# A segment mean over sorted ids: probes and gathers ordered later in the queues, id sums fewer rows ahead

## The chip, the core and the metric

The kernel runs on one core of a Trainium2 chip. The metric is the device time of one execution in microseconds (us). A core has five engines with a queue each: TensorE (PE), VectorE (DVE), ScalarE (ACT), GpSimd (POOL) and SyncE (SP), which here only issues transfers. The transfers of all queues run on the core's 16 DMA engines.

## The reference

```python
n, num_segments = 10_000_000, 10000
data = randn(n).astype(float32)
segment_ids = sort(randint(0, num_segments, n))          # int64

sums = zeros(num_segments); counts = zeros(num_segments)
np.add.at(sums, segment_ids, data)
np.add.at(counts, segment_ids, 1)
return sums / maximum(counts, 1)
```

The ids are sorted, so each segment is one contiguous run of about 1,000 elements. Data is 40 MB; the ids would be 80 MB, and the kernel does not read them all.

## The kernel before

**Tiling.** Each of the 128 partitions holds 78,125 consecutive elements, worked on as 90 rows of 875 (the last has 250). A row holds at most one place where the id changes, or a general path is taken at the end (it is not, with this data). For each row the kernel needs the sum of all its elements (T), the place of the change (KK), and the sum of the elements before that place (A). The segment sums then come from scans over these per-row numbers.

**The steps of a row, and where they run.**
- *Probes* (load_probes, L156, on SP): every 175th id, 8 bytes each, loaded for a group of six rows at once; 15 groups, 128 x 30 ids each.
- *Data* (load_data, L163, on SP): tiles of two rows, 875 KB; 18 buffers. Before a buffer is loaded anew SP waits for its readers.
- *First look* (L253, DVE): once a group; five or six small steps find from the probes which window of 175 ids of each row holds the change, and write its index (IDX). It ends with the six gathers of the group.
- *Gather* (L299, POOL): an indirect load of the window's ids, 128 x 175, one for each row, into GT, a ring of 18.
- *Id sum* (add_ids, L310, ACT): adds the ids of one window. Rows 87 to 89 are summed together on DVE (add_ids_late, L316).
- *Second look* (L322, DVE): turns a group's id sums into KK.
- *Total* (L333, ACT): adds up a row's data. *Split* (L339, DVE): adds up the data before KK.

**The order** is written out by hand. A loop over r from -40 to 89 (L846) emits the work, and each queue runs its part in this order. At each r come: the probe loads that are X_PROBE + X_DATA rows ahead, the data loads that are X_DATA rows ahead, id sums up to X_SUM rows ahead of the total, the total and split of row r, and then all steps that `put(r, steps, every)` has listed under `after[r]`, `every` of them a row from r on. So on SP only the order of probe and data loads counts: the probes of group g stand just before the tile of rows 6g-14 and 6g-13. A first look stands after row 6g-12, its second look after row 6g-1. SP's loads each wait also for the one eight loads before, since eight completion semaphores are used in turn.

**The late work** also hangs on `put`. Counts, sums, select and table (L556, L586, L651, L660) turn rows of T, A and KK into segment means for parts of the rows; keys (L454) and edges_of (L440) prepare ids; check, single and verdict (L485, L538, L546) test that the fast path holds; pick (L688) makes masks, on DVE for rows 62 to 77 and on POOL for the rest; spread (L739) multiplies by these masks, total_of (L751) adds them up, weights (L713) and finish (L757) close. The sums and spread of rows 62 to 77 stand after row RM = 78, those of rows 78 to 83 after row RE = 84 and the one after it, the rest after row 88. The last first look (rows 84 to 89) stands after row 72, together with counts of rows 62 to 77.

The lines that place the looks and the id sums:

```python
put(a - 1, second_look(a, b))                                   # L792
put(max(bounds[g] - X_LOOK, 0), first_look(g), 5)               # L795
while r >= -1 and gs < min(r + 1 + X_SUM, IDS):                 # L864
    add_ids(gs)
```

Of the kernel before, what the change touches and what calls it, by code (L numbers as in the profile page):

```python
# [22 lines left out]
NR = 90  # L23
# [4 lines left out]
NX = NR + E  # L28
FAR = float(1 << 18)
GROUPS = [6] * 15  # L30
X_PROBE = 14
X_DATA = 26
X_LOOK = 12
X_SUM = 7
RING = 18
IDS = 87
NO = 79
SHIFT = 6
ND = 2 * SHIFT + 1
# [2 lines left out]
R1 = 8 * M1 - 2  # L42
R2 = NR + 4
RM = 78
RE = 84
C1, CA, C2 = 37, 70, 51


# [69 lines left out]
def kernel(  # L118
# [6 lines left out]
    nc = tc.nc  # L125
# [13 lines left out]
    ppool = ctx.enter_context(tc.tile_pool(name="ppool", bufs=1, space=bass.MemoryType.PSUM))  # L139

    ctx.enter_context(tc.manual_schedule())


    pr = cpool.tile([P, NR + 1, K], I64, name="pr")
# [171 lines left out]
    def add_ids_late(r):  # L316
        n, q = NR - r, r % RING
        nc.vector.tensor_reduce(  # L318
            out=GS[:, r:NR], in_=gt32[:, q : q + n, 0 : 2 * W : 2], axis=AX.X, op=ALU.add
        )  # L320

    def second_look(a, b):  # L322
        def s1():
            nc.vector.scalar_tensor_tensor(  # L324
                out=KK[:, a:b], in0=YY[:, a:b], scalar=float(S // K), in1=GS[:, a:b],
                op0=ALU.mult, op1=ALU.subtract,
            )
            if b == NR:
                nc.vector.tensor_add(out=KK[:, NR - 1 : NR], in0=KK[:, NR - 1 : NR], in1=tl)

        return [s1]
# [35 lines left out]
    pb = cpool.tile([P, NO - C2, R2 - RM], FP32, name="pb")  # L367
# [86 lines left out]
    def keys(a, b):  # L454
        def s1():
            if a == 0:
                nc.vector.tensor_add(out=base1, in0=VI[:, 0:1], in1=pin)

        def s2():
            v = VI[:, a:b] if b <= NR else V[:, a:b]  # L460
            nc.vector.tensor_scalar(
                out=KEY[:, PAD + a : PAD + b], in0=v, scalar1=base1[:, 0:1], scalar2=None, op0=ALU.subtract
            )
            if b <= NR:
                edges(a, b)
            if a == 0:
                nc.vector.tensor_sub(out=delta, in0=sp, in1=base1)

        def s3():
            if b <= NR:  # L470
                nc.vector.tensor_scalar(
                    out=NB[:, a:b], in0=BT[:, a:b], scalar1=1.0, scalar2=None, op0=ALU.not_equal
                )
            if a == 0:
                nc.vector.tensor_scalar(
                    out=dm, in0=jj[:, 0:ND], scalar1=delta[:, 0:1], scalar2=None, op0=ALU.is_equal
                )

        def s4():
            if b <= NR:  # L480
                positions(a, b)

        return [s1, s2, s3, s4]
# [204 lines left out]
    def pick(e, o, c0, n, a, b):  # L688

        w = b - a  # L690

        def s1():
            c = min(b, NR)
            e.tensor_scalar(
                out=KL[:, a - R1 : c - R1], in0=VI[:, a:c], scalar1=sp[:, 0:1], scalar2=None, op0=ALU.subtract
            )
            if c < b:
                e.tensor_scalar(
                    out=KL[:, c - R1 : b - R1], in0=V[:, c:b], scalar1=sp[:, 0:1], scalar2=None,
                    op0=ALU.subtract,  # L700
                )

        def s2():
            k, j = view(KL[:, a - R1 : a - R1 + 1], [[0, n], [1, w]]), view(jj[:, c0 : c0 + 1], [[1, n], [0, w]])
            if e is nc.vector:
                e.tensor_tensor(out=o, in0=k, in1=j, op=ALU.is_equal)  # L706
            else:
                e.tensor_tensor(out=o, in0=k, in1=j, op=ALU.subtract)
                e.tensor_scalar(out=o, in0=o, scalar1=0.0, scalar2=None, op0=ALU.is_equal)  # L709

        return [s1, s2]
# [68 lines left out]
    def put(r, steps, every=1):  # L780
        for i, f in enumerate(steps):
            after[r + i // every].append(f)
# [3 lines left out]
    after[-1] += second_look(0, GROUPS[0])  # L786
    for a, b in zip(bounds[1:], bounds[2:]):
        if b == NR:
            put(a - 2, second_look(a, IDS))
            put(a - 1, [lambda: add_ids_late(IDS)] + second_look(IDS, b), 2)  # L790
        else:
            put(a - 1, second_look(a, b))  # L792
    for g in range(HEAD, NG):
        if g < NG - 1:
            put(max(bounds[g] - X_LOOK, 0), first_look(g), 5)  # L795
# [1 line left out]
    def mixed(p, q):  # L797
        out = []
        for i in range(max(len(p), len(q))):
            out += p[i : i + 1] + q[i : i + 1]  # L800
        return out
# [15 lines left out]
    put(41, counts(0, Q1), 2)  # L817
    put(45, sums(0, Q1) + select(0, H1) + table(0, H1, tab), 2)
    put(52, [lambda: nc.sync.dma_start(out=out2d[0:SHIFT, :].rearrange("n u -> u n"), in_=tab[0:1, 0:SHIFT])])
    put(56, keys(48, 72)[1:], 2)  # L820
    put(59, counts(Q1, R1), 2)
    put(R1 - 1, mixed(sums(Q1, R1), select(H1, M1)) + table(H1, M1, tab), 2)
    put(64, place(0, T1, tab, [(0, C1, ND + 1, OUT[:, 0:C1]), (C1, T1, ND + 1, xa[:, 0 : T1 - C1, RM - R1])]))
    put(67, mixed(keys(72, RE)[1:], pick(nc.vector, pa[:, :, 0 : RM - R1], C1, CA - C1, R1, RM)), 2)
    put(69, check())
    look = bounds[NG - 1] - X_LOOK
    put(RM - 11, pick(nc.gpsimd, pb[:, :, 0 : RE - RM], C2, NO - C2, RM, RE), 2)
    put(look, mixed(first_look(NG - 1), counts(R1, RM)), 99)
    put(look, pick(nc.gpsimd, pb[:, :, RE - RM :], C2, NO - C2, RE, R2), 99)
    put(look + 1, mixed(edges_of(RE, NR), []), 99)  # L830
    put(look + 2, single(RE, NR, bad[:, 2 * NX + 8 :]) + verdict()[:1], 99)
    put(look + 3, verdict()[1:])
    after[look + 4].append(lambda: verdict_reg.append(nc.values_load(badi[0:1, 0:1], min_val=0, max_val=1)))
    put(RM, sums(R1, RM, False) + spread(R1, RM, pa[:, :, 0 : RM - R1], xa[:, :, 0 : RM - R1], CA - C1, nc.gpsimd), 4)
    put(RM + 4, total_of(xa[:, 0 : C2 - C1, :], OUT[:, C1:C2])
        + total_of(xa[:, C2 - C1 :, :], add[:, 0 : CA - C2, nb]), 2)
    put(RE, mixed(counts(RM, R2), sums(RM, RE, False)), 99)
    put(RE + 1, mixed(spread(RM, RE, pb[:, :, 0 : RE - RM], add[:, :, 0 : RE - RM], NO - C2), weights()), 99)
    put(NR - 2, sums(RE, R2, False, NR - 1)
        + spread(RE, R2, pb[:, :, RE - RM :], add[:, :, RE - RM : nb], NO - C2) + total_of(add, most), 99)  # L840
    assert max(after) <= NR - 1

    pnext = 0
# [2 lines left out]
    for r in range(-X_PROBE - X_DATA, NR):  # L846
        while pnext < NG and bounds[pnext] <= r + X_PROBE + X_DATA:
            load_probes(pnext)
            pnext += 1
            if pnext == 1:  # L850
                load_data(0)
                nt = 1
        while nt < NT and 2 * nt <= r + X_DATA:
            load_data(nt)
            nt += 1
        if r == -X_DATA:
            nc.scalar.dma_start(
                out=snt[0 : P - 1, :],
                in_=segment_ids[D : N].rearrange("(p d) -> p d", d=D)[:, 0:1],
            )  # L860
        if r == -1:
            for f in after[r][: 5 * HEAD]:
                f()
        while r >= -1 and gs < min(r + 1 + X_SUM, IDS):  # L864
            add_ids(gs)
            gs += 1
        if r == -1:
            for f in after[r][5 * HEAD :]:
                f()
        if r >= 0:  # L870
            total(r)
            split(r)
            for f in after[r]:
                f()
# [31 lines left out]
```

## Time and profile before

| what | us |
|---|---|
| median of 4 runs (lowest, highest) | 192.76 (192.18, 193.32) |
| the profiled execution | 191.72 |
| its span, first to last instruction | 189.9 |
| DVE busy | 141.6 (75%) |
| ACT busy | 135.2 (71%) |
| POOL busy | 99.0 (52%) |
| PE busy | 1.6 (1%) |
| one split of 875 elements, DVE | 1.12 |
| one total, ACT (with the read of its sum) | 0.93 + 0.19 |
| one id sum, ACT (with the read of its sum) | 0.36 + 0.19 |
| one gather's issue, POOL | 1.00 |

The page divides the span into 40 slices of 4.75 us; a digit is the busy share of a slice in tenths, 9 being 90% or more. The DMA row is the mean over 16 engines. In the list of waits a line reads: who waited, for whom, total us, times, longest. In the timeline a line reads: start, us, engine, line, operation, output and inputs with their shapes, and in brackets the idle time before it and what ended it. A DMA issued by POOL stands in the timeline with the time POOL needs to issue it; the landing comes later.

### The profile page before, as it was taken

The numbers are of one execution on the slowest core, as the hardware profiler recorded it, in microseconds if no ns is written. First come the engines' busy times: TensorE is split into PE (matmuls) and PEld (weight loads), VectorE is DVE, ScalarE is ACT, GpSimd is POOL, SyncE is SP. The second block draws the span as 40 slices with busy tenths as digits, with TensorE's granted clock in tenths as the row PEclk, the third lists the DMA queues.
The fourth block names the chain that finished last, engine by engine and source line by source line (L and its number), as shares of the span: only waits on it lengthen the run. The fifth ranks groups of instructions, "written<-read, shape, count | busy, mean of one in ns | idle before, by whom it ended". The sixth has DMA issues, their size and how long they took to land.

```text
span 189.9 us, 1435 instructions
## 1 busy us (share of the span) xinstructions
PE 1.6 (1%) x6; PEld 1.4 (1%) x6; DVE 141.6 (75%) x438; ACT 135.2 (71%) x356; POOL 99.0 (52%) x119
## 2 busy tenths in 40 slices
PE   0000000000001000000000000000000001000000
PEld 0000000000001000000000000000000001000000
DVE  6530684976785848849499995758969999799990
ACT  8012289999998859859497696768859659699700
POOL 5577875667556272663716537273570776750000
DMA  6999999999999999999999999999999999996000
GB/s 24 178 188 219 403 378 224 406 260 352 396 192 399 271 313 403 201 402 240 361 382 215 412 190 396 343 252 412 197 402 284 334 410 397 410 409 238 0 0 10
DMA packets 70164, 54.62 MB, mean 288 GB/s; under 512 B 60016, under 2 KB 60584, under 8 KB 70151
## 3 DMA queue, kind: packets, MB, share of 16 engines
q1 hardware_dynamic: 64219, 40.50, 72.0%
q0 software_dynamic: 5760, 14.01, 22.7%
q14 instruction: 13, 0.11, 0.2%
q10 hardware_dynamic: 172, 0.00, 0.1%
HBM read 56.59 MB, written 0.04 MB: 298 GB/s over the span
## 4 chain that ended last, share of the span: by engine, by line
SPq 34%; DMA 31%; DVE 17%; issue 8%; ACT 5%; POOL 1%; POOLq 0%; ACTq 0%; DVEq 0%
SPq L167 30%; DMA data_t<-in_data_dram 23%; DVE junk_v L342 10%; DMA GT<-in_segment_ids_dram,IDX 8%; SPq L159 4%; ACT junk_a L337 3%; ACT junk_a L311 2%; POOL GT L301 1%; DVE shf L677 0%; DVE q L589 0%; DVE add L745 0%; DVE FFP L595 0%; DVE most L753 0%; DVE GS L318 0%; DVE pa L706 0%
## 5 line engine op out<-in xcount | busy, mean ns | idle before, releaser
L301 POOL DMA_INDIRECT GT<-in_segment_ids_dram,IDX x90 | 90.1, 1001 | 67.3 <-ACT junk_a L337 28.0
L342 DVE SCALAR_TENSOR_TENSOR junk_v<-iota,q,data_t 128x875 bf16<-128x875 f32 x90 | 100.7, 1119 | 23.0 <-DMA data_t<-in_data_dram 21.8
L337 ACT ACTIVATE junk_a<-data_t 128x875 bf16<-128x875 f32 x90 | 83.6, 929 | 19.7 <-DMA data_t<-in_data_dram 17.1
L311 ACT ACTIVATE junk_a<-GT 128x175 bf16<-128x175 int32 x87 | 31.3, 360 | 23.8 <-DMA GT<-in_segment_ids_dram,IDX 21.3
L337 ACT ACTIVATION_READ_ACCUMULATOR junk_a<-data_t 128x1 f32 x90 | 16.8, 186 | 0.0
L311 ACT ACTIVATION_READ_ACCUMULATOR junk_a<-GT 128x1 f32 x87 | 16.2, 186 | 0.0
L324 DVE SCALAR_TENSOR_TENSOR q<-YY,GS 128x6 f32<-128x6 f32 (+1 forms) x16 | 2.6, 161 | 10.2 <-ACT junk_a L311 10.2
L342 DVE DVE_READ_ACCUMULATOR junk_v<-iota,q,data_t 128x1 f32 x90 | 7.5, 83 | 0.0
L268 DVE TENSOR_REDUCE SG<-pr 128x6 f32<-128x30 int32 x15 | 2.7, 181 | 5.2 <-DMA pr<-in_segment_ids_dram 5.2
L183 ACT ACTIVATE GT<-q 128x3150 int32<-128x3150 f32 x1 | 3.0, 3002 | 0.0
L277 DVE TENSOR_SCALAR far<-ST 128x6 f32<-128x6 f32 x15 | 2.6, 171 | 0.5
L284 DVE SCALAR_TENSOR_TENSOR IDX<-ST,wb 128x6 int32<-128x6 f32 (+2 forms) x16 | 2.5, 161 | 0.5
L271 DVE SCALAR_TENSOR_TENSOR ST<-pr,SG 128x6 f32<-128x6 int32 x15 | 2.5, 165 | 0.5
L280 DVE TENSOR_TENSOR ST<-ST,far 128x6 f32<-128x6 f32 x15 | 2.5, 165 | 0.5
L287 DVE SCALAR_TENSOR_TENSOR YY<-ST,SG 128x6 f32<-128x6 f32 x15 | 2.4, 159 | 0.0
L589 DVE TENSOR_TENSOR q<-T,q 128x44 f32<-128x44 f32 (+4 forms) x5 | 1.2, 242 | 1.2 <-ACT junk_a L337 1.0
L232 DVE CAST jj<-jj_i 128x128 f32<-128x128 int32 x1 | 1.5, 1483 | 0.7 <-POOL jj_i L231 0.7
L183 ACT ACT_TABLE_LOAD x1 | 1.3, 1283 | 0.7 <-PEq L890 0.7
L709 POOL TENSOR_SCALAR pb<-pb 128x168 f32<-128x168 f32 (+1 forms) x2 | 1.6, 790 | 0.2
L549 PE MATMUL badp<-bads,ones 128*128 128x1 f32 x2 | 0.6, 362 | 102.9 <-DVE bads L548 102.9
L595 DVE TENSOR_TENSOR_SCAN FFP<-NBP,FFP,XX 128x44 f32<-128x44 f32 (+4 forms) x5 | 1.3, 264 | 0.1
L662 DVE TENSOR_TENSOR sel<-sel,RF 128x280 f32<-128x280 f32 (+1 forms) x3 | 1.2, 408 | 0.1
(128 smaller groups left out, 45.0 us busy)
## 6 DMA issues: line engine op xcount, KB each, us to landing
data_t<-in_data_dram SPq DMA_DIRECT2D x44, 875.0 KB, 10.3
GT<-in_segment_ids_dram,IDX POOLq DMA_INDIRECT x90, 6.6
data_t<-in_data_dram SPq DMA_DIRECT2D x1, 437.5 KB, 17.1
pr<-in_segment_ids_dram SPq DMA_DIRECT2D x13, 30.0 KB, 12.2
data_t<-in_data_dram SPq DMA_DIRECT2D x1, 125.0 KB, 14.6
out_dram<-OUT SPq DMA_DIRECT2D x1, 36.6 KB
pr<-in_segment_ids_dram SPq DMA_DIRECT2D x1, 31.0 KB
pr<-in_segment_ids_dram SPq DMA_DIRECT2D x1, 26.0 KB
```

The lines of the kernel that those rows point to most:

```text
L159: nc.sync.dma_start(out=pr_flat[:, a:b], in_=ids_p[:, a * S : (b - 1) * S + 1 : S])
L167: nc.sync.dma_start(out=d[:, 0 : c - a], in_=data_p[:, a:c])
L183: nc.scalar.activation(out=gt32[:, :, 0 : 2 * W : 2], in_=view(q5[:, 0, 0:1], [[0, RING], [0, W]]), func=ACT.Copy)
L268: v.tensor_reduce(out=SG[:, a:b], in_=pr32[:, a:b, 0 : 2 * K : 2], axis=AX.X, op=ALU.add)
L271: v.scalar_tensor_tensor(out=ST[:, a:b], in0=VI[:, a + 1 : b + 1], scalar=float(K), in1=SG[:, a:b], op0=ALU.mult, op1=ALU.subtract,)
L277: v.tensor_scalar(out=far, in0=ST[:, a:b], scalar1=0.0, scalar2=FAR, op0=ALU.is_equal, op1=ALU.mult)
L280: v.tensor_add(out=ST[:, a:b], in0=ST[:, a:b], in1=far)
L301: nc.gpsimd.indirect_dma_start(out=GT[:, r % RING, :], out_offset=None, in_=ids2d[:], in_offset=bass.IndirectOffsetOnAxis(ap=IDX[:, r : r ...
L311: nc.scalar.activation(out=junk_a[:, 0:W], in_=gt32[:, r % RING, 0 : 2 * W : 2], func=ACT.Copy, accum_out=GS[:, r : r + 1],)
L324: nc.vector.scalar_tensor_tensor(out=KK[:, a:b], in0=YY[:, a:b], scalar=float(S // K), in1=GS[:, a:b], op0=ALU.mult, op1=ALU.subtract,)
L337: nc.scalar.activation(out=junk_a[:, 0:n], in_=d, func=ACT.Copy, accum_out=t)
L342: nc.vector.scalar_tensor_tensor(out=junk_v[:, 0:n], in0=iota[:, 0:n], scalar=KK[:, r : r + 1], in1=d, op0=ALU.is_lt, op1=ALU.mult, accum_ ...
```

## The change

X_PROBE goes from 14 to 11 and X_LOOK from 12 to 9. Probe loads are moved behind two data loads in SP's queue. First looks and the gathers that they issue stand after row 6g-9. Id sums run 6 rows ahead of the totals for rows under 66 and 4 rows ahead from there (at most 7 before). From row 66 on a group has two second looks of three rows each. Several late steps move down by 2 to 4 rows: check from after row 69 to 73, keys and the masks of rows 62 to 77 from 67 to 70, the last first look and what hangs on it (counts, edges, single, verdict) by three rows, the sums of rows 62 to 77 from 78 to 80, those that began after row RE = 84 to after row RS = 86, where they now take in rows 84 and 85.

```diff
--- before.py
+++ after.py
@@ -28,12 +28,12 @@
 NX = NR + E
 FAR = float(1 << 18)
 GROUPS = [6] * 15
-X_PROBE = 14
+X_PROBE = 11
 X_DATA = 26
-X_LOOK = 12
-X_SUM = 7
+X_LOOK = 9
 RING = 18
 IDS = 87
+HALVES = 66
 NO = 79
 SHIFT = 6
 ND = 2 * SHIFT + 1
@@ -43,6 +43,7 @@
 R2 = NR + 4
 RM = 78
 RE = 84
+RS = 86
 C1, CA, C2 = 37, 70, 51
 
 
@@ -139,6 +140,9 @@
     ppool = ctx.enter_context(tc.tile_pool(name="ppool", bufs=1, space=bass.MemoryType.PSUM))
 
     ctx.enter_context(tc.manual_schedule())
+
+    def x_sum(r):
+        return 6 if r < HALVES else 4
 
 
     pr = cpool.tile([P, NR + 1, K], I64, name="pr")
@@ -786,10 +790,13 @@
     after[-1] += second_look(0, GROUPS[0])
     for a, b in zip(bounds[1:], bounds[2:]):
         if b == NR:
-            put(a - 2, second_look(a, IDS))
-            put(a - 1, [lambda: add_ids_late(IDS)] + second_look(IDS, b), 2)
+            put(a - 1, second_look(a, IDS))
+            put(IDS - 2, [lambda: add_ids_late(IDS)] + second_look(IDS, b), 2)
+        elif a < HALVES:
+            put(a - 1, second_look(a, b))
         else:
-            put(a - 1, second_look(a, b))
+            put(a - 1, second_look(a, a + 3))
+            put(a + 2, second_look(a + 3, b))
     for g in range(HEAD, NG):
         if g < NG - 1:
             put(max(bounds[g] - X_LOOK, 0), first_look(g), 5)
@@ -817,27 +824,27 @@
     put(41, counts(0, Q1), 2)
     put(45, sums(0, Q1) + select(0, H1) + table(0, H1, tab), 2)
     put(52, [lambda: nc.sync.dma_start(out=out2d[0:SHIFT, :].rearrange("n u -> u n"), in_=tab[0:1, 0:SHIFT])])
-    put(56, keys(48, 72)[1:], 2)
+    put(58, keys(48, 72)[1:], 2)
     put(59, counts(Q1, R1), 2)
     put(R1 - 1, mixed(sums(Q1, R1), select(H1, M1)) + table(H1, M1, tab), 2)
     put(64, place(0, T1, tab, [(0, C1, ND + 1, OUT[:, 0:C1]), (C1, T1, ND + 1, xa[:, 0 : T1 - C1, RM - R1])]))
-    put(67, mixed(keys(72, RE)[1:], pick(nc.vector, pa[:, :, 0 : RM - R1], C1, CA - C1, R1, RM)), 2)
-    put(69, check())
+    put(70, mixed(keys(72, RE)[1:], pick(nc.vector, pa[:, :, 0 : RM - R1], C1, CA - C1, R1, RM)), 2)
+    put(73, check())
     look = bounds[NG - 1] - X_LOOK
-    put(RM - 11, pick(nc.gpsimd, pb[:, :, 0 : RE - RM], C2, NO - C2, RM, RE), 2)
+    put(70, pick(nc.gpsimd, pb[:, :, 0 : RE - RM], C2, NO - C2, RM, RE), 2)
     put(look, mixed(first_look(NG - 1), counts(R1, RM)), 99)
     put(look, pick(nc.gpsimd, pb[:, :, RE - RM :], C2, NO - C2, RE, R2), 99)
     put(look + 1, mixed(edges_of(RE, NR), []), 99)
     put(look + 2, single(RE, NR, bad[:, 2 * NX + 8 :]) + verdict()[:1], 99)
     put(look + 3, verdict()[1:])
     after[look + 4].append(lambda: verdict_reg.append(nc.values_load(badi[0:1, 0:1], min_val=0, max_val=1)))
-    put(RM, sums(R1, RM, False) + spread(R1, RM, pa[:, :, 0 : RM - R1], xa[:, :, 0 : RM - R1], CA - C1, nc.gpsimd), 4)
-    put(RM + 4, total_of(xa[:, 0 : C2 - C1, :], OUT[:, C1:C2])
+    put(RM + 2, sums(R1, RM, False) + spread(R1, RM, pa[:, :, 0 : RM - R1], xa[:, :, 0 : RM - R1], CA - C1, nc.gpsimd), 4)
+    put(RM + 5, total_of(xa[:, 0 : C2 - C1, :], OUT[:, C1:C2])
         + total_of(xa[:, C2 - C1 :, :], add[:, 0 : CA - C2, nb]), 2)
-    put(RE, mixed(counts(RM, R2), sums(RM, RE, False)), 99)
-    put(RE + 1, mixed(spread(RM, RE, pb[:, :, 0 : RE - RM], add[:, :, 0 : RE - RM], NO - C2), weights()), 99)
-    put(NR - 2, sums(RE, R2, False, NR - 1)
-        + spread(RE, R2, pb[:, :, RE - RM :], add[:, :, RE - RM : nb], NO - C2) + total_of(add, most), 99)
+    put(RS, mixed(counts(RM, R2), sums(RM, RS, False)), 99)
+    put(RS + 1, mixed(spread(RM, RS, pb[:, :, 0 : RS - RM], add[:, :, 0 : RS - RM], NO - C2), weights()), 99)
+    put(NR - 2, sums(RS, R2, False, NR - 1)
+        + spread(RS, R2, pb[:, :, RS - RM :], add[:, :, RS - RM : nb], NO - C2) + total_of(add, most), 99)
     assert max(after) <= NR - 1
 
     pnext = 0
@@ -861,7 +868,7 @@
         if r == -1:
             for f in after[r][: 5 * HEAD]:
                 f()
-        while r >= -1 and gs < min(r + 1 + X_SUM, IDS):
+        while r >= -1 and gs < IDS and gs <= r + x_sum(gs):
             add_ids(gs)
             gs += 1
         if r == -1:
```

## The prediction

> **What bounds the kernel now.** I read the page from the slices (part 2) to the DMA queues (part 3), then busy time in stretches, the waits, and the timeline of the last 50 us. The page first:
>
> ```profile
> span 189.9 us, 1435 instructions
> ...
> DVE  6530684976785848849499995758969999799990
> ...
> DMA  6999999999999999999999999999999999996000
> ...
> q1 hardware_dynamic: 64219, 40.50, 72.0%
> q0 software_dynamic: 5760, 14.01, 22.7%
> ```
>
> The 16 DMA engines are full from the second slice to the 36th: q1 (data and probes) and q0 (gathers) fill 94.7% of the span. DVE is full only at the end. Summed by size, the trace's packets take 100.8 us of 16 engines for data (7,000 B packets), 43.1 us for 90 gathers (0.48 us each) and 33.8 us for 57,216 probe packets of 8 B (2.26 us for each of 15 probe loads). The change leaves all of these as they are and moves only their order. The stretches (busy us of PE, PEld, DVE, ACT, POOL; clock, DMA share, GB/s):
>
> ```profile
> 120.00:130.00 10.00, 0.00 (x0) 0.00 (x0) 6.81 (x21) 7.39 (x21) 5.77 (x6) 1.00 1.08 304
> 140.00:150.00 10.00, 0.00 (x0) 0.00 (x0) 9.69 (x27) 8.86 (x24) 3.93 (x5) 1.00 1.02 316
> 150.00:160.00 10.00, 0.00 (x0) 0.00 (x0) 9.90 (x46) 6.76 (x18) 7.25 (x9) 1.00 1.01 399
> 170.00:175.00 5.00, 0.00 (x0) 0.00 (x0) 4.90 (x13) 4.84 (x11) 0.00 (x0) 1.00 0.77 304
> 175.00:180.00 5.00, 0.00 (x0) 0.00 (x0) 4.93 (x21) 4.27 (x10) 0.00 (x0) 1.00 0.00 0
> ```
>
> Two regimes: up to about 140 us DVE has gaps and follows the data; from 140 us DVE has none to speak of and sets the end. Data ends at 174.8 us, DVE at 185.7: a backlog of 10.9 us. Only an earlier start of the second regime, or work or idle time taken out of it, shortens the kernel. The waits (total us, times, longest) and five rows of the timeline:
>
> ```profile
> DVE junk_v L342 <- DMA data_t<-in_data_dram: 21.8, 14, 2.6
> ACT junk_a L311 <- DMA GT<-in_segment_ids_dram,IDX: 21.3, 13, 8.5
> DVE q L324 <- ACT junk_a L311: 10.2, 3, 6.0
> ```
>
> ```profile
> 157.73 1.10 POOL L301 DMA_INDIRECT GT<-in_segment_ids_dram,IDX  x1 [1.31 <-ACT junk_a L311]
> ...
> 158.92 1.12 DVE L342 SCALAR_TENSOR_TENSOR junk_v<-iota,q,data_t 128x875 bf16<-128x875 f32 x1
> ...
> 164.71 0.36 ACT L311 ACTIVATE junk_a<-GT 128x175 bf16<-128x175 int32 x1 [1.46 <-DMA GT<-in_segment_ids_dram,IDX]
> ...
> 166.25 0.52 DVE L589 TENSOR_TENSOR q<-T,q 128x16 f32<-128x16 f32 x1 [1.05 <-ACT junk_a L337]
> ...
> 185.45 0.25 DVE L762 SCALAR_TENSOR_TENSOR OUT<-wp,q,most 128x28 f32<-128x28 f32 x1
> ```
>
> 158.92 is the split of row 74. The other rows show one late wait: gather 84 lands late, ACT stands 1.46 us at its sum, row 77's total comes late, and the sums of rows 62 to 77 stop DVE for 1.05 us.
>
> **Probes later (lead 11).** On SP each probe load passes two data loads: that of group g goes from before the tile of rows 6g-14, 6g-13 to before that of rows 6g-10, 6g-9. The tiles passed land 2.26 us earlier; tiles of rows 2 and 3 of a group of six gain nothing. First looks run after row 6g-9, whose tile is queued behind the probe, so no probe comes too late.
>
> **Gathers later (look lead 9).** The first look of a group (5 or 6 small DVE steps, 1.0 us) and its six POOL gathers run three rows later. Then fewer gathers lie ahead of any data tile, at 0.48 us each. By tile, from the trace's landings:
> - Row 62: 135.23 now. The gathers 66 to 71 start 1.6 us after row 57 ends, about 126.0 instead of 122.70; 2.9 fewer have landed, 1.4 us: 133.85.
> - Row 64: 140.11 now; 1.4 us for gathers and 2.26 us for the probe: 136.5.
> - Row 68 (behind its probe in both): 146.39 now. Gathers 72 to 77 start after row 63 (136.5 + 1.6) at 138.1 instead of 134.52; 3.1 fewer, 1.5 us: 144.9.
> - Row 74 (likewise): 157.26 now. Rows 68 and 69 have no side work left, so row 69 ends at 147.3 and gather 78 starts at 148.9, only 1.65 us after the present 147.25. Some 1.8 fewer have landed, 0.85 us: 156.4.
>
> So DVE starts row 64 3.6 us earlier. It reaches row 68 at about 143.0 (4.3 us for rows 64, 65; 0.9 for the first look gone from row 66, 0.4 for keys gone from row 67) and waits until 144.9. Rows 68 to 73 are six at 1.1 us, a first look 0.95, keys and mask 1.2, check's first step 0.46, a second look 0.1: 9.3, thus 154.2. There it waits 2.2 us for row 74.
>
> **Side work later.** What crosses row 74 is then paid behind its tile: check's second and third steps 0.44 + 0.78, the last first look with counts 1.54 (155.59 to 157.13), edges 0.74 (158.18 to 158.92): 3.5 us. From row 74 to the last result there are 26.78 us now (158.92 to 185.70); less 1.13 us idle at the sums (they now run after row 80, when row 77's total is some 5 us old): 25.65. Add 3.5 and 0.16 for extra second looks; take off 0.12 us for each of three bare row boundaries that these fill, and 0.01 for spreads of 8 and 8 rows instead of 6 and 10: 28.94. **156.4 + 28.94 = 185.35**, against 185.70.
>
> **New waits at the end.** The last first look ends at about 161.1, gather 84 starts at 161.9, 4.2 us later than 157.73. Three deadlines come close:
> - Gather 86 (164.5 + 7.3) lands at 171.8, ACT has summed it at 172.8, and the second look after row 83 wants it at 172.9. Behind it in DVE's queue is row 84.
> - POOL's last masks (2.4 us now) follow gather 89 and end at 171.9, then the spread into xa (1.24) ends at 173.1; DVE's reductions want it at 172.9 or 173.0.
> - Gather 89 (168.4 + 7.0) lands at 175.4; the late sum after row 85 wants it at 175.9.
>
> I price the three together at 0.35 us; the bounds are 0 and 2.5 us (each gather half as slow again as its row). End: 185.7, as before. The 4.2 us behind it are unchanged, so is the 1.8 us between span and the profiled execution's 191.72. That execution lies 1.0 us under the median of 192.76; the difference of the two kernels, 0.0, is put on the median: **192.8**.
>
> **Ids summed 6 rows ahead.** Here a rule is to be weighed. The row is the tile view of GT:
>
> ```profile
> DMA to landing us min/median/max: 3.2/6.6/7.5
> ```
>
> The Trainium skill ("DMA: Bandwidth & Descriptors", Anatomy of one DMA, SWDGE path) fits such a DMA with 2.0 us plus bytes over 436 GB/s: an estimate of 2.4 us for these 179 KB. From the end of row 6g-9 the sixth gather starts at 8.1 us; by the rule it lands at 10.5 and the group's second look runs at about 12, well ahead of row 6g's data at 15.9 (five tiles at 3.2 us and one probe, less two rows). By the trace gathers land at 7.1, 9.9, 11.1, 12.6, 13.5 and 14.4, and since ACT takes one total (1.0 us) and one id sum (0.5) in turn from the second one on, the second look runs at 15.3 to 16.9: up to 1 us late at every boundary of rows 18 to 65. I take the trace, since its engines are full. DVE then does rows 6g to 6g+1 while the next tile still waits behind a probe (3.2 + 2.26 us), so data catches it again: cost nothing, with 1.9 us of cover at row 68; without that cover, 1 us a group. In the first groups the wait is longer (row 18 about 2.4 us late by the same steps, row 24 0.4). ACT has room, 7.4 us busy in ten; its totals hold only sums and buffers.
>
> **Threes and lead 4 from row 66.** Three more DVE steps of about 0.08 us, counted above. The first three of a group need only its third gather, 3.9 us sooner.
>
> **Rivals.**
> - The lead carries through. If row 74's tile came with the 3 us that row 64 has (more gathers deferred than I count), the end would be 185.7 - 3.6 - 1.05 + 0.3 = 181.3, 188.4 us. For it: DVE waits 21.8 us on data now. Against it: full engines, and work is only passed to and fro. Half of it, 190.6, is as likely as all.
> - Gathers become the bound (slower). At boundaries of rows 18 to 65, DVE stands on ACT's id sums. Price: up to 1 us for each of 8 groups. It decides once DVE reaches row 68 later than 144.9, so from 1.9 us of accumulated delay; at half the price, 4 us - 1.9 = +2.1: 194.9. Its late twin (gathers 86 and 89) gives up to +2.2 by the bound above. For it: the sums of gathers are waited for in both the second and third wait rows. Against it: the probe behind row 6g+1.
> - Nothing moves but the order, the forecast.
>
> **Numbers.** What this kernel's measurement can tell from no change is 0.5%, 0.96 us. The forecast has 0.46 (own range 191.8 to 193.8: row 74's tile by 0.6 either way, the waits by 0.35), the lead 0.24, gathers 0.30. Faster takes the lead and a little of the forecast, 0.26; slower 0.31; same 0.43. The range, 190.7 to 195.0, reaches half the lead and the gathers at half price.
>
> **What would show it.** Right: DVE waits on data at rows 68 and 74 of about 2 us each; row 74 starts near 156.4; no 1 us wait before the sums; gather 84 starts near 162; data ends at 174 to 175. Wrong: row 74 below 155 (the lead), or DVE waiting on ACT's id sums by more than 1 us at many boundaries, or for GT or xa after row 83 by over 1 us; or data that ends later than 175.5, which the fixed DMA work does not allow for.

## Result and the profile after

The changed kernel takes **192.0 us** in the median (34 runs, 191.06 to 193.84); the kernel before, run beside it, 192.9 us (55 runs, 191.52 to 197.8). The ratio is 0.9967, 95% interval 0.995 to 0.9983: faster by a third of a per cent. That is inside the half per cent that the prediction called no change, but the interval leaves out 1, so the change is real and small. The forecast was 192.8. The ratios here and below leave out the slow runs, those over 1.5% above the fastest of the same kernel; the medians hold all runs.

The profiled execution of the changed kernel, 193.17 us (span 191.4), is 1.2 us above its own median, and that of the kernel before, 191.72 us, was 1.2 us below its median. So the two given profiles, set side by side, show the changed kernel slower by 1.45 us, while 89 runs show it faster, by 0.6 us (by the ratio) to 0.9 us (by the medians). Differences of this size can't be read from one profile of each. The page of the changed kernel:

```profile
span 191.4 us, 1427 instructions
...
DVE  6530297979196975975799885795897969999991
...
DMA  6999999999999999999999999999999999996000
...
q1 hardware_dynamic: 64219, 40.50, 71.8%
q0 software_dynamic: 5760, 14.01, 23.9%
```

Same transfers, same digits for the DMA engines. Of DVE's last slices, the 33rd (153.1 to 157.9 us) is a 6 where it was a 9: that is the wait at row 74. The stretches:

```profile
140.00:150.00 10.00, 0.00 (x0) 0.00 (x0) 8.76 (x23) 7.02 (x19) 6.10 (x6) 1.00 1.07 309
150.00:160.00 10.00, 0.00 (x0) 0.00 (x0) 8.30 (x29) 8.40 (x23) 7.38 (x9) 1.00 1.07 307
170.00:175.00 5.00, 0.00 (x0) 0.00 (x0) 4.81 (x12) 4.41 (x12) 4.40 (x6) 1.00 1.00 394
175.00:180.00 5.00, 0.00 (x0) 0.00 (x0) 4.89 (x13) 4.84 (x10) 0.00 (x0) 1.00 0.10 33
```

In 150 to 160 us DVE was busy for 9.90 us before and is for 8.30 now. The side work that filled this stretch is gone from it, and it is paid later. The waits (total, times, longest):

```profile
DVE q L328 <- ACT junk_a L315: 27.0, 11, 8.7
ACT junk_a L315 <- DMA GT<-in_segment_ids_dram,IDX: 25.3, 22, 4.0
...
DVE junk_v L346 <- DMA data_t<-in_data_dram: 6.9, 6, 2.2
```

Waits on data fell from 21.8 to 6.9 us, and waits of the second looks on id sums rose from 10.2 to 27.0. Three rows of the timeline carry the end:

```profile
157.82 1.13 DVE L346 SCALAR_TENSOR_TENSOR junk_v<-iota,q,data_t 128x875 bf16<-128x875 f32 x1 [1.70 <-DMA data_t<-in_data_dram]
...
163.62 1.10 POOL L305 DMA_INDIRECT GT<-in_segment_ids_dram,IDX  x1 [3.56 <-DVE IDX L288]
...
187.09 0.25 DVE L766 SCALAR_TENSOR_TENSOR OUT<-wp,q,most 128x28 f32<-128x28 f32 x1
```

The first is the split of row 74. Its tile stands in SP's queue behind the last probe load (3,328 packets), and DVE waits for it for 1.70 us. From there it is 29.51 us to the last result, where the kernel before needs 26.78.

### The profile page after: what moved, and what is told of

The parts are those of the page before. It is cut to its first block, busy times and chain, and to the rows that moved or that the text cites. A ratio compares the mean times of both kernels' runs of the same rounds, so it can differ in the third digit from the quotient of the medians.

```text
span 191.4 us, 1427 instructions
## 1 busy us (share of the span) xinstructions
PE 1.6 (1%) x6; PEld 1.4 (1%) x6; DVE 142.7 (75%) x441; ACT 135.2 (71%) x356; POOL 99.8 (52%) x119
## 4 chain that ended last, share of the span: by engine, by line
DMA 43%; issue 21%; DVE 16%; ACT 13%; POOL 5%; POOLq 0%; ACTq 0%; DVEq 0%
DMA GT<-in_segment_ids_dram,IDX 23%; DMA data_t<-in_data_dram 20%; DVE junk_v L346 8%; ACT junk_a L341 7%; ACT junk_a L315 6%; POOL GT L305 4%; DVE q L328 1%; DVE jj L236 1%; POOL i_i L198 0%; DVE add L749 0%; DVE FFP L599 0%; DVE most L757 0%; DVE GS L322 0%; POOLq L305 0%; DVE add L757 0%
## 5 line engine op out<-in xcount | busy, mean ns | idle before, releaser
L328 DVE SCALAR_TENSOR_TENSOR q<-YY,GS 128x6 f32<-128x6 f32 (+1 forms) x19 | 3.9, 207 | 27.0 <-ACT junk_a L315 27.0
L599 DVE TENSOR_TENSOR_SCAN FFP<-NBP,FFP,XX 128x8 f32<-128x8 f32 (+3 forms) x5 | 1.3, 254 | 0.1
L553 PEld LDWEIGHTS badp<-bads,ones 128*128 128x128 f32 x2 | 0.5, 312 | 107.1 <-DVE bads L552 107.1
```

The costliest lines, as they stand in the source:

```text
L328: nc.vector.scalar_tensor_tensor(out=KK[:, a:b], in0=YY[:, a:b], scalar=float(S // K), in1=GS[:, a:b], op0=ALU.mult, op1=ALU.subtract,)
```

## The experiments

The first theory, called the gate theory in the expectations, was the prediction's own picture: the tile of row 74 sets the time of the changed kernel, and side work moved behind it is paid in full. The rival was that the end does not matter so much as what happens upstream, in the queues and at the looks. Each kernel was compared with runs of the kernel before on the same chip; that kernel's median was 192.1 to 192.9 us in these comparisons, so across experiments the ratios compare better than the times. Below, "row n" is the start of the split of row n on DVE, and "the end" is the end of the last result.

### How much one profile says: both kernels profiled twice more

Nothing is changed in these.

> The kernel before, profiled once more, because its profile (191.72 us) lies 1.2 us under its median and that of the changed kernel (193.17) 1.2 us over its own. Gate theory (the tiles of rows 68 and 74, each queued behind a probe load, hold DVE, and what DVE does after the row 74 tile sets the end): from the landing of the row 74 tile to the last DVE result about 28.4 us again (157.26 to 185.70), whatever the draw. Rival (the end follows the id sums in the middle): the stretch from the row 74 tile to the end varies with the draw as the waits for id sums do.

> The kernel before, a third profile, for the spread of its draws: row 64 started at 140.14 and 141.84 us in the two so far, and the ends were 185.70 and 186.89. If the draw of row 64's tile sets before's time, the end is 45.0 to 45.6 us after the start of row 64 again.

> The changed kernel once more: 192.0 us, 0.3% under before. Gate theory: DVE starts row 74 within 0.2 us of its tile's landing, after a wait of 1 us or more, and ends 29.0 to 29.6 us later. Rival: no such wait at row 74, DVE comes late to it from waits for id sums.

> The changed kernel, a third profile: row 74 started at 157.82 and 156.77 us in the two so far, after waits of 1.70 and 2.37 us, and the ends came 29.51 and 29.23 us later. Gate theory: a wait of over 1 us at row 74 again and an end 29.1 to 29.6 us behind it.

| kernel, profiled execution | us | row 64 (wait) | row 74 (wait) | end |
|---|---|---|---|---|
| before, given | 191.72 | 140.14 (1.52) | 158.92 (0) | 185.70 |
| before, second | 192.74 | 141.84 (3.39) | 160.63 (0) | 186.89 |
| before, third | 195.45 | 144.02 (3.85) | 162.79 (0) | 189.55 |
| changed, given | 193.17 | 139.23 (0) | 157.82 (1.70) | 187.33 |
| changed, second | 191.89 | 138.06 (0) | 156.77 (2.37) | 185.99 |
| changed, third | 191.73 | 138.11 (0) | 156.78 (2.41) | 185.90 |

The second profile of the changed kernel belongs to a timed run: 191.88 us, ratio 0.9974 (0.9948 to 1.0). Row 64 of the kernel before in its third profile, from the timeline:

```profile
144.02 1.13 DVE L342 SCALAR_TENSOR_TENSOR junk_v<-iota,q,data_t 128x875 bf16<-128x875 f32 x1 [3.85 <-DMA data_t<-in_data_dram]
```

In the kernel before the end follows row 64 by 45.05 to 45.56 us each time, and DVE waits for that row's tile each time. So this one start, which spreads over 3.9 us, sets the time. The expectation for the second profile had named the wrong tile: DVE doesn't wait at row 74 in this kernel, and in the third profile the end comes 29.28 us after the landing of row 74's tile (160.27), not 28.4. In the changed kernel row 64 comes 3.5 us earlier (means 138.5 and 142.0), but the end follows row 74, by 29.11 to 29.51 us.

The means of three profiles give the account of the change. Row 74 starts at 160.8 before and at 157.1 now, a gain of 3.7 us; from there to the end it takes 26.6 us before and 29.3 now, a loss of 2.7. The end moves from 187.4 to 186.4, by 1.0 us, near the 0.6 to 0.9 of the timed runs.

### The gate at row 74: side work moved back ahead of it

To the changed kernel:

```diff
-    put(70, mixed(keys(72, RE)[1:], pick(nc.vector, ...)), 2)
-    put(73, check())
+    put(67, mixed(keys(72, RE)[1:], pick(nc.vector, ...)), 2)
+    put(69, check())
```

> The changed kernel with check after rows 69 to 71 and keys and masks from row 67 as before the change; nothing else. Gate theory: 1.2 us of DVE work (check's second and third steps) goes from behind the row 74 tile into the wait ahead of it (1.70 us in the changed kernel's profile): 190.8 to 191.2 us, 0.4 to 0.6% under the changed kernel, and DVE ends about 28.2 us after the row 74 tile. Rival (id sums): DVE has the same work and the same waits for id sums, 191.8 to 192.2 us.

Measured: 190.25 us, ratio 0.9886 (0.9837 to 0.9935). That is 1.6 us, 0.8%, under the changed kernel of the same comparison (191.88), and more than the 0.4 to 0.6% expected. Row 74 in its timeline:

```profile
155.75 1.13 DVE L346 SCALAR_TENSOR_TENSOR junk_v<-iota,q,data_t 128x875 bf16<-128x875 f32 x1 [0.66 <-DMA data_t<-in_data_dram]
```

From there 28.32 us to the end, as the gate theory expected (28.2). The steps of check now fill time in which DVE stood waiting, and are no longer paid behind it: 0.8 to 1.2 us less than in the three profiles of the changed kernel. So the gate is real. The other part of this profile's lead is that row 74 itself starts 1.0 us earlier than in the second and third profile, though DVE waits for its tile here too. The gate theory has nothing for that, and one profile can't tell it from chance.

### The looks of the middle groups put back

To the changed kernel; the looks of groups from row 66 on stay as they are:

```diff
-            put(max(bounds[g] - X_LOOK, 0), first_look(g), 5)
+            put(max(bounds[g] - (12 if bounds[g] < HALVES else X_LOOK), 0), first_look(g), 5)
```

> The changed kernel with first looks of the groups under row 66 twelve rows ahead as before, nine from row 66 on. Gate theory: DVE's waits for id sums (27.0 us in the changed kernel) fall below 12 us, waits for data rise by about as much, the tiles of rows 68 and 74 land as before, and the time stays within 0.4 us of the changed kernel: 191.6 to 192.4 us. Rival (id sums are the bound now): at least 1 us faster than the changed kernel, 191.0 us or less.

Measured: 189.93 us, ratio 0.9857 (0.9816 to 0.9899). The gate theory missed: nothing was done at row 74, where DVE still waits, and yet the kernel gained about 1%.

```profile
156.04 1.13 DVE L346 SCALAR_TENSOR_TENSOR junk_v<-iota,q,data_t 128x875 bf16<-128x875 f32 x1 [2.57 <-DMA data_t<-in_data_dram]
```

Row 64 came at 135.98, 2.1 to 3.3 us earlier than in the changed kernel. The rival of this expectation, id sums, has the time right, and the waits for them did fall, from 27.0 to 11.7 us. But the edit also changes what is in flight together, as the next two experiments show, so it doesn't decide between the two.

Both edits together, and then also the last first look placed after row 73 instead of 75:

```diff
-    put(look, mixed(first_look(NG - 1), counts(R1, RM)), 99)
+    put(look - 2, first_look(NG - 1), 99)
+    put(look, counts(R1, RM), 99)
```

> Both single edits that were faster, together: first looks twelve rows ahead for groups under row 66, and check after rows 69 to 71 with keys from row 67. Gate theory: in the profile with the first edit alone DVE stood 2.57 us at the row 74 tile; 1.2 us of work fits into it: 1.0 to 1.2 us faster than that edit alone (189.9), 188.7 to 189.0 us. Rival (both edits draw on the same waits, so that only one of them counts): 189.6 to 190.2 us.

> The same with the last first look (rows 84 to 89) after row 73 by itself, its counts left after row 75. Gate theory: 0.5 us less DVE work behind the row 74 tile, and the gathers 84 to 89 start some 4 us sooner, so that the wait for the id sum of row 86 and for xa after row 83 (0.5 us in the changed kernel) goes: 0.5 to 1.0 us faster than the two edits alone, about 188.1 us. Rival: the two steps no longer run interleaved and cost what they save: no change against the two edits alone.

Measured: 188.78 us (0.9796, 0.9769 to 0.9824) and 188.34 us (0.9777, 0.9749 to 0.9804). The two gains nearly add up (3.1 us under 191.88, against 1.6 and 1.9 alone), and with the third edit the wait at row 74 is gone (row 74 at 155.48, 26.89 us to the end).

### One constant alone

The kernel before with nothing but the probe lead of 11, and the changed kernel with nothing but the old lead of 14:

```diff
-X_PROBE = 14
+X_PROBE = 11
```

> The kernel before with X_PROBE = 11 and nothing else. Gate theory: the tile of row 64 no longer stands behind a probe load (about 2 us earlier), that of row 68 does instead; DVE is held at row 68 (tile at about 146.4 in the profile of before, where it started the row at 147.9) and the end moves forward by about 1.5 us: 190.6 to 191.6 us where before has 192.1. First looks wait for their probes on DVE, at no cost, since the next tile waits behind the same probe. Rival (id sums bound, and only their order matters): first looks wait up to 2 us a group and the time is that of before or more, 192.0 to 194 us.

> The changed kernel with X_PROBE = 14 as before: looks, sums and late work moved, probes not. Gate theory: the tiles behind probes are those of rows 64 and 70 instead of 68 and 74; row 70 starts at about 149.7 and is followed by 34.7 us of DVE work less the wait, the end comes near 185 us: 191.0 to 192.0 us, that is, between 0.8 us faster than and equal to the changed kernel (191.9). Rival (id sums): the same waits for id sums as in the changed kernel (27 us), and the same time within 0.3 us.

Measured: 188.96 us, ratio 0.9823 (0.9789 to 0.9858), and 190.85 us, ratio 0.9898 (0.9869 to 0.9927). The first is faster than either theory allowed, the second a little faster. **Probes three rows later alone gain 1.8%; all the rest of the change without it gains 1.0%; together they gain 0.3%.** Rows 64 and 74 of the first kernel:

```profile
137.52 1.13 DVE L342 SCALAR_TENSOR_TENSOR junk_v<-iota,q,data_t 128x875 bf16<-128x875 f32 x1
...
156.83 1.12 DVE L342 SCALAR_TENSOR_TENSOR junk_v<-iota,q,data_t 128x875 bf16<-128x875 f32 x1
```

No wait at either: row 64 is 4.5 us ahead of the mean of before. Row 74 starts no earlier than in the changed kernel, but from there to the end it takes 26.26 us where the changed kernel takes 29.11 to 29.51. So the 3 us by which this kernel beats the changed one are spent behind row 74, where the change has put its late work.

The 4 us by which it beats the kernel before arise ahead of row 64. What ran on the DMA engines there differs. One microsecond a line, the kernel before (third profile) behind a probe load; the last two columns are the DMA share and GB/s:

```profile
136.00:137.00 1.00, 0.00 (x0) 0.00 (x0) 0.99 (x5) 0.49 (x3) 0.91 (x1) 1.00 1.45 40
137.00:138.00 1.00, 0.00 (x0) 0.00 (x0) 1.00 (x3) 0.82 (x1) 0.69 (x2) 1.00 0.88 52
138.00:139.00 1.00, 0.00 (x0) 0.00 (x0) 0.96 (x5) 0.94 (x5) 0.70 (x2) 1.00 0.88 198
139.00:140.00 1.00, 0.00 (x0) 0.00 (x0) 0.97 (x4) 0.97 (x3) 0.69 (x2) 1.00 0.74 231
```

and the kernel with the probe lead of 11 alone:

```profile
127.00:128.00 1.00, 0.00 (x0) 0.00 (x0) 0.96 (x3) 0.45 (x2) 0.70 (x2) 1.00 1.43 154
128.00:129.00 1.00, 0.00 (x0) 0.00 (x0) 0.93 (x6) 0.38 (x2) 0.69 (x2) 1.00 1.21 126
129.00:130.00 1.00, 0.00 (x0) 0.00 (x0) 1.00 (x2) 0.97 (x3) 0.74 (x1) 1.00 1.16 176
130.00:131.00 1.00, 0.00 (x0) 0.00 (x0) 0.02 (x2) 0.94 (x5) 0.00 (x0) 1.00 1.13 349
```

In the first, 8-byte probes run nearly alone (40 GB/s), and then the engines are partly empty for 3 us (shares of 0.74 to 0.88). In the second, probes and gathers run side by side (126 to 176 GB/s), and the share stays above 1. From the start and duration of every packet I counted how many were in flight. What is missing from 16, over 20 to 150 us, is in the table of the next experiment as "engines empty".

### Is it the phase between probes and gathers?

Groups have six rows, so what is in flight together should depend on the probe lead less the look lead, modulo six; I call this the phase. It was 14 - 12 = 2; in the changed kernel it is 11 - 9 = 2 again; in the two kernels with one constant altered it is 11 - 12 and 14 - 9, both 5. If that is the cause, a lead longer by three must be fast as well, and one longer by six slow.

```diff
-X_PROBE = 14
+X_PROBE = 17
```

> The kernel before with probes 17 rows ahead instead of 14, and nothing else. What is tested is why 11 was worth 4 us. Phase theory: what counts is where the probe packets run against the gathers, that is probe lead less look lead, modulo the six rows of a group; 17 less 12 is 5, as 11 less 12 is, so this kernel is fast too: 188.5 to 190.5 us, ratio 0.98 to 0.988, and under 2 us between 20 and 165 us in which only probe packets are in flight (before: 9.5). Rival, the lead itself: a later probe lets tiles go ahead of it, so an earlier probe costs what the later one gained: 193 us or more, ratio 1.0 to 1.02.

The same with 20, and the changed kernel with 17:

> The kernel before with probes 20 rows ahead. 20 less 12 is 8, which is 2 modulo six, the phase of before. Phase theory: 192 to 194 us, ratio 0.995 to 1.005, and 8 to 11 us with only probe packets in flight. Rival, the lead: slower still than 17 rows, over 194 us. Second rival, any lead other than 14 is better (14 has some private clash with a wait on SP): 190 us or less.

> The changed kernel with probes 17 rows ahead instead of 11: 17 less 9 is 8, 2 modulo six, the phase of the changed kernel itself (11 less 9), while 14 less 9 gave 190.85 us. Phase theory: 191.5 to 193 us, and 6 to 9 us with only probe packets in flight. Rival: the earlier the probes the better in the changed kernel, since its looks come late: 190.5 us or less.

| kernel | probe and look lead | phase | us | ratio (95%) | engines empty, us | row 64 |
|---|---|---|---|---|---|---|
| before | 14, 12 | 2 | 192.9 | 1 | 3.6, 4.5, 4.4 | 140.1, 141.8, 144.0 |
| before, probes 20 | 20, 12 | 2 | 194.09 | 1.0097 (1.0063 to 1.0131) | 4.0 | 142.8 |
| changed | 11, 9 | 2 | 192.0 | 0.9967 (0.995 to 0.9983) | 2.5, 2.5, 2.1 | 139.2, 138.1, 138.1 |
| changed, probes 17 | 17, 9 | 2 | 190.94 | 0.9924 (0.9894 to 0.9954) | 1.3 | 139.5 |
| before, probes 11 | 11, 12 | 5 | 188.96 | 0.9823 (0.9789 to 0.9858) | 0.3 | 137.5 |
| before, probes 17 | 17, 12 | 5 | 190.24 | 0.9894 (0.9863 to 0.9924) | 0.3 | 139.0 |
| changed, probes 14 | 14, 9 | 5 | 190.85 | 0.9898 (0.9869 to 0.9927) | 0.4 | 139.2 |
| changed, middle looks back | 11, 12 | 5 | 189.93 | 0.9857 (0.9816 to 0.9899) | 1.1 | 136.0 |

In the kernel before, leads of 11, 14, 17 and 20 go fast, slow, fast, slow: no steady rise or fall with the lead gives that. At equal phase the lead costs 1.3 us for six rows (11 to 17) and 1.2 to 1.9 (14 to 20, by the medians or by the ratio), and the phase some 3 us. The ratios of the first two runs lie a little above the ranges that the phase theory gave (0.9894 over 0.988, 1.0097 over 1.005). The third run missed by 0.6 us. Its row 64 is no earlier than the changed kernel's, as the phase says, but its last probe load stands before the tile of row 68, and with it the gate at row 74 is gone (row 74 at 155.50 with no wait, 29.44 us to the end). I had left that out of the expectation.

Two things weaken the case for the phase. First, with looks 9 rows ahead the phase doesn't show in the time: probes 17 (phase 2) and 14 (phase 5) take the same 190.9 us, and in both the wait at row 74 is gone. Second, the slow leads of the kernel before, 14 and 20, are also those whose probe load stands just before the tile of row 64, for which DVE then waits. The changed kernel with probes 14 has that place too, in the good phase, and it waits there:

```profile
139.15 1.13 DVE L346 SCALAR_TENSOR_TENSOR junk_v<-iota,q,data_t 128x875 bf16<-128x875 f32 x1 [2.18 <-DMA data_t<-in_data_dram]
```

What speaks for the phase apart from any one tile is the work of all transfers together. With each kind of packet at its mean cost in the given profile of before, the kernels of the table with phase 5 had done 155.4 to 156.1 us of transfer work by 150 us, this last one included, and those with phase 2 had done 152.0 to 154.3. So the phase goes with faster transfers; how much of the 3 us is the phase and how much the place of row 64's probe load is not separated.

### By what does the phase act? Probe loads cut in two

I had taken it for a stall on SP: the issue of the data load behind a probe load takes some 10 us, and then the engines run dry. From group 3 on, each probe load is cut into two of 1,920 packets, the first one tile earlier:

```diff
+    halves = [(bounds[g], g, None) for g in range(3)]
+    for g in range(3, NG):
+        halves += [(bounds[g] - 2, g, 0), (bounds[g], g, 1)]
...
-        while pnext < NG and bounds[pnext] <= r + X_PROBE + X_DATA:
-            load_probes(pnext)
+        while pnext < len(halves) and halves[pnext][0] <= r + X_PROBE + X_DATA:
+            load_probes(*halves[pnext][1:])
```

> The kernel before with each probe load from group 3 on cut in two loads of 1,920 packets, the first one tile earlier (a data tile stands between them). The work of the DMA engines is the same. Tested is the step behind the phase: that 3,840 packets of 8 bytes hold up SP's next data load until they are nearly drained, so that the engines run dry behind them. If so, two halves hold it up half as long, and a tile waits between them: under 5 us with only probe packets in flight between 20 and 165 us (before: 9.5), row 64 starts at 137.5 to 139.5 (140.1 to 144.0 in three profiles of before), 189 to 191.3 us. Rival: what costs is that probes and gathers do not coincide, whatever the size of a load; half loads spread out coincide no better: 192 to 193.5 us, and 8 to 11 us of probes alone.

> The changed kernel with the same cut of each probe load in two. If large probe loads run the engines dry: under 4 us of probes alone (changed kernel: 6.5 to 8), row 64 at 136 to 137.5 (138.1 to 139.2 now); of that gain the gate at row 74, behind a half load only, gives back less than now: 188.5 to 190.5 us. Rival (only coincidence with gathers counts): 191.3 to 192.5 us.

Measured: 192.12 us, ratio 1.0012 (0.9985 to 1.0038), and 191.68 us, ratio 0.9971 (0.9942 to 1.0001). The cut did what it should on SP. Its queue in the kernel before (start, us to issue):

```profile
102.59 11.41 SPq L167 DMA_DIRECT2D data_t<-in_data_dram  x3
114.05 0.44 SPq L159 DMA_DIRECT2D pr<-in_segment_ids_dram  x1
114.59 10.56 SPq L167 DMA_DIRECT2D data_t<-in_data_dram  x3
```

and with the loads cut:

```profile
113.96 6.13 SPq L169 DMA_DIRECT2D data_t<-in_data_dram  x1
120.14 0.43 SPq L161 DMA_DIRECT2D pr<-in_segment_ids_dram  x1
120.67 4.79 SPq L169 DMA_DIRECT2D data_t<-in_data_dram  x2
```

Time with no packet over 8 bytes in flight, probes alone in the main, fell from 9.5 to 2.7 us (between 20 and 165 us), and no time was gained: my theory missed. The kernel with the probe lead of 11 alone shows the same from the other side. It is fast, and its SP is held as long as that of the kernel before:

```profile
119.34 0.42 SPq L159 DMA_DIRECT2D pr<-in_segment_ids_dram  x1
119.87 10.06 SPq L167 DMA_DIRECT2D data_t<-in_data_dram  x3
```

**So neither the stall on SP nor the time of probes alone decides.** The cut has side effects, though: it shifts half of the probes by two rows, and with five loads to six rows instead of four, the rule that a load waits for the one eight loads before lets SP run less far ahead. Either may hide a gain. The rival got the time right and the probes wrong, so it isn't shown either. The engines were still empty for 2.7 us (before 3.6 to 4.5), and a data packet took 289 ns on average. That mean is 277 to 280 ns in the four kernels of phase 5 in the table and 282 to 290 in all kernels of phase 2. The phase therefore shows in longer data packets and, less sharply, in empty engines (the changed kernel with the cut has 1.1 us of them, as much as one kernel of phase 5); why packets grow longer stays open.

In the changed kernel the cut moved row 64, and the gate swallowed it:

```profile
136.35 1.12 DVE L348 SCALAR_TENSOR_TENSOR junk_v<-iota,q,data_t 128x875 bf16<-128x875 f32 x1
...
156.81 1.13 DVE L348 SCALAR_TENSOR_TENSOR junk_v<-iota,q,data_t 128x875 bf16<-128x875 f32 x1 [1.30 <-DMA data_t<-in_data_dram]
```

Row 64 is 1.7 us earlier than in the second and third profile of the changed kernel, row 74 starts where it did (156.8), and so does the end (186.03).

### What of the change is worth keeping

Probes 11 rows ahead in the kernel before, and the sums of rows 62 to 77 two rows later as in the change:

```diff
-    put(RM, sums(R1, RM, False) + spread(...), 4)
-    put(RM + 4, total_of(...)
+    put(RM + 2, sums(R1, RM, False) + spread(...), 4)
+    put(RM + 5, total_of(...)
```

> The probe move alone, and the sums of rows 62 to 77 after row 80 instead of 78 (reductions after row 83 instead of 82), as the change has it. Gate theory: no work crosses a tile that DVE waits for, and the wait for row 77's total ahead of the sums (0.6 to 1.1 us) goes: 188.0 to 188.5 us, 0.3 to 0.6% under the probe move alone. Rival (that wait is covered): 188.7 to 189.3 us.

Measured: 187.77 us, ratio 0.9772 (0.9726 to 0.9818), a little under the range expected and some 2% under the changed kernel. With its interval it is level with the 188.34 us (0.9777) of the three edits above; the kernel gets there with two. Row 74 to the end takes 25.85 us, as the prediction's 25.65 for this had it.

One run told little. It has the probe lead of 11, check and keys after rows 73 and 70, and the verdict three rows later:

> The kernel with the probe move alone, and of the late work only what the change does with check and keys: check from after row 69 to 73, keys and masks from 67 to 70 (verdict three rows later, so that it still follows check). Gate theory: 1.2 us of check goes behind the row 74 tile; with the probe move alone DVE met that tile 0.3 us after its landing, so 0.9 us is lost: 189.6 to 190.2 us against 189.0 for the probe move alone. Rival (the order of side work on DVE is free, only transfers and id sums count): 188.7 to 189.3 us.

By the code, the edges written after row 73 are read by the last steps of check after row 75, which take them for a failure of the fast path; the program took its general path and 186,276 us. Up to the last result of the fast path, at 183.46 us, its profile is usable: row 74 at 156.83 without a wait and 26.63 us to the end. Against the probe lead alone (183.09, 26.26) the work moved across row 74 cost 0.4 us where 0.9 was expected, but a difference of that size can't be read from one profile of each.

## Why the prediction was right and wrong

**Right: the new end.** The sum put row 74 at 156.4 with a wait of 2.2 us and 28.94 + 0.35 us behind it, an end of 185.7. Two of three profiles have 156.8 with waits of 2.4, 29.11 and 29.23 us, and ends of 185.90 and 185.99; in the given one row 74 is 1.0 us later and the end 1.4. That side work which crosses row 74 is paid is shown by the edit that moved check back. The idle 1.13 us at the sums is gone.

**Right by luck: the gain at row 64**, 3.6 us forecast, 3.5 between the means. Both ends of the difference were some 2 us too early: 140.11 for the kernel before is the earliest of three, with a mean of 142.0, and the changed kernel has 138.1 to 139.2 where 136.5 was forecast. Its tile landed at 138.3 (given) and 137.2 (third), and DVE came to it later still. **Too large, for this reason: the wait at row 68**, 1.9 us forecast, 1.00, 0.54 and 0.48 measured.

**Right in kind: the three late edges.** Gather 84 started at 163.6 (third profile 162.2) instead of 161.9. In the given profile the second look after row 83 took 0.67 us where such steps take 0.15, a wait of 0.5 us; 0.35 was taken for all three. One sign of being wrong came true there: data ended at 176.4, later than 175.5. In the third profile it ended at 175.0, and the kernel before varies more (174.8 and 178.3).

**Wrong: the step from profile to median,** "the difference of the two kernels, 0.0, is put on the median". This is the step that missed the gain. The 0.0 compares a new end with one execution of the kernel before, in which row 64's tile landed at 140.1; in two more it came at about 141.7 and 143.9. From the end to the profiled time it is 5.8 to 6.0 us in all six profiles, so the median of 192.9 belongs to an end near 187.0. Against that, 185.7 is a gain of 1.3 us; 0.6 to 0.9 was measured. In the terms of the sum, the start of row 74 was to move by 2.5 us (158.92 to 156.4) and the work behind it to grow by 2.5; between the means of three profiles the first is 3.7, since before's mean is 160.8, and the second 2.7. The prediction saw that the profile lay 1.0 us under its median, and gave that 1.0 to both kernels. But the spread is that of the kernel before: its ends lie 3.9 us apart, those of the changed kernel 1.4.

**Wrong: "The change leaves all of these as they are and moves only their order."** The packets are the same, the time they need is not. By the count above, the kernel before had done 152.0 to 153.9 us of transfer work by 150 us in three profiles; with the probe lead of 11 alone it had done 155.9. A digit of 9 or a share of 1.0 in the page covers this: 16 engines were never empty for long, but 3.6 to 4.5 us in all were missing. The rival "the lead carries through" was dismissed with "full engines, and work is only passed to and fro", and the argument for that was this step. In the change itself this step did no harm: the changed kernel had done 152.7 to 153.8. Moving probes and looks by the same three rows leaves their phase where it was, so the forecast was saved by the change, not by its argument.

**Open: "Ids summed 6 rows ahead ... cost nothing".** The waits came, 27.0 us instead of 10.2, and at 2.5 us each (27.0 over 11) larger than the 1 us a group that was forecast. The prediction was right to take the slow landing of gathers from the trace: in the changed kernel it is 6.9 us in the median (3.4 to 8.2). Nine of the eleven were over 1 us, which the prediction had named as a sign of being wrong, for the rival that gathers become the bound; yet the kernel was not slower. The waits took the place of waits on data (21.8 to 6.9), as argued. But putting the middle looks back alters the ids' slack and the phase at once, and with the old probe lead these waits fall to 16.5 us with the ids as in the change, so no run prices them alone.

## What to carry to other kernels

If one landing sets the end, take several profiles of the kernel before you subtract from it: here three of them lay 3.9 us apart, and the whole change was worth under 1. When two kinds of transfers recur with the same period, vary the lead of one against the other over a whole period, and don't move both together: with looks 12 rows ahead the offset went with 3 us, the lead with some 0.2 us a row. Before moving filler work later, look for the wait that it fills; behind a gate it is paid.

## What was not expected of the hardware

- The same packets in another order left the DMA engines empty for less time: 0.3 to 1.1 us in 130 in all kernels of phase 5, 3.6 to 4.5 in the kernel before.
- Data packets of 7,000 bytes took 276 to 280 ns on average in the kernels of phase 5 and 282 to 290 in those of phase 2; gather packets went the other way, 135 to 140 ns against 120 to 131. Probe packets stayed at 9.2 to 9.9 ns.
- The DMA share rose above 1 (1.45 at 40 GB/s) where nearly all packets in flight had 8 bytes, so the share said little of use there.
- The issue of the data load behind 3,840 small packets held SP's queue for about 10 us, behind 1,920 for 3 to 6, and yet halving the load gained nothing. That was no wait for a free buffer: in the kernel before, the load for rows 58 and 59 was held from 114.59 to 124.20 us, and the last readers of its buffer (row 23, 18 tiles earlier) were done at 61.8.
